# Fillers around the indexer's scores: 24 matmuls ahead of them, five in place of three beside each

## The chip, the cores and the metric

The kernel runs on one core of one Trainium2 chip. The metric is the device time of one execution in microseconds (us), as a median of several runs. The engines are called as in the profile: PE is the matrix engine (TensorE), PEld its weight loads, DVE is VectorE, ACT is ScalarE, POOL is GpSimd and SP is SyncE, which issues most transfers.

## What is computed

One transformer block on 512 tokens of width 1024, all in float32. The part that matters here is the token mixing:

```
q_a,k_a,v_a, q_i,k_i,w_i, q_s,k_s,v_s, g_a,g_b = split(x @ w_in)
# indexer: a score of each key for each query, and its 128 best keys
dots  = einsum('thd,sd->ths', q_i, k_i) * 64**-0.5
score = einsum('th,ths->ts', w_i, relu(dots))            # chunk-causal
sel   = top_k(score, 128)
# branch A: softmax attention over the selected keys, with a relative bias
# branch B: stick-breaking attention, strictly causal
merged = sigmoid(g_a)*(y_a @ w_branch_dsa) + sigmoid(g_b)*(y_s @ w_branch_sb)
x = layer_norm(alpha*x + merged @ w_out)
# then a gated MLP with a causal convolution and a second layer norm
```

Each branch has 8 heads of 64 channels; the indexer has 8 heads of 64.

## The kernel before, in words

**Products.** Each weight and activation is split into a high part (`hi`, made by ACT) and a low part (`lo`, made by DVE, or by POOL or an accumulating transfer for some tiles), and a product is three matmuls: hi by hi, hi by lo, lo by hi. `Stream` loads the weights tile by tile in a fixed order over SP's queue and splits each three tiles ahead of its use (L101 for `whi`, L107 for `wlo`).

**Stages up to the attention.** The indexer's queries are projected while x arrives (L300 to L302). Then come its keys (`idx_keys`, L359), and its scores (`idx_scores`, L377): for each of the query blocks 1, 2 and 3 and each of 8 heads two matmuls of 256, 384 or 512 columns into a PSUM bank `dot_ps` (L385, L386), a relu on ACT (L388) and a multiply and add on DVE (L391, L393). That makes 24 scores of two matmuls. Block 0 has no more than 128 keys and needs none. The top-k of a block (`select`, 16 rounds of a max L402 and a replace L403) runs on DVE. Block 1's rounds are asked for one by one during the scores of blocks 2 and 3; the others behind the scans of the stick-breaking heads (`ROUNDS`).

**Fillers.** All other projections of the token mixing are a list of filler tiles, `FILL` (L33): the stick-breaking values `vs`, then `qs0 ks0 qs1 ks1 qs2 ks2 gb0 gb1` and so on, the sparse branch's values `va`, the output products of branch B (`bs0` to `bs3`) and gates `ga`. A tile of q, k, gate or branch is 24 matmuls of 512 columns; the rest of `vs` is 72 here and `va` 96. `fill(n)` (L607) advances the list by steps of three matmuls until at least n are asked for, so `fill(3)` is one step, `fill(5)` two, `fill(24)` eight. `fill_until(name)` (L614) advances it until a tile is done. Only places in the program move by it: the list and its total stay the same.

**Heads.** `start_head` (L644) asks for a head's q and k tiles and its logits (`z_ps` L503, or `l_ps` for the sparse heads). For a stick-breaking head follow sigmoids on ACT, four scans on DVE (`sb_sticks`, L517), a product on POOL (L519), ten transposes on PE (`tr_ps`, L429), their split (L432, L433) and the product with the values (`av_ps`, L476). Between these steps `fill(GAP)` asks for 15 fillers. The eight sparse heads follow, with the top-k mask added on POOL (`bm`, L532). The values `va` are forced by `fill_until("va")` (L658) at the first of them.

**PSUM.** There are eight banks: four behind `pa` and four behind `pb`. The scores, the keys, all q, k and gate tiles, `va` and `bs` take theirs from `pa`; `vs`, the heads' logits, transposes and products from `pb`.

**What sets the order.** The kernel is built with a planner (L1216, `schedule_with_timeline_sim=True`): it runs the program against its own model of time and puts into each engine's queue, among the instructions that are ready in that model, the one that stands first in the program; `issue_after` ties some behind others. On the chip each queue then runs in that order. So a filler can stand ahead of a score that the program asks for earlier, when the score was not ready in the model, and a place in the program is a priority and not an order.

Of the kernel before, what the change touches and what calls it, by code (L numbers as in the profile page):

```python
# [121 lines left out]
def tile_block(ctx: ExitStack, tc: tile.TileContext, xT, xN, w_qi, w_ki, w_t, w_v, w_br, w_o, w_fi, w_fo,  # L122
# [27 lines left out]
    def pa(name):  # L150
        return psA.tile([128, 512], F32, tag="A", name=name)
# [225 lines left out]
    def idx_scores():  # L377
        kih, kil, wi = index["k"]
        for j in (1, 2, 3):
            N = 128 * (j + 1)  # L380
            for h in range(H):
                yield j
                ps = pa("dot_ps")
                r = slice(j * 128, j * 128 + 128)
                nc.tensor.matmul(ps[:, :N], qi[h][:, r], kih[:, :N], start=True, stop=False)  # L385
                nc.tensor.matmul(ps[:, :N], qi[h][:, r], kil[:, :N], start=False, stop=True)  # L386
                rl = bp.tile([128, 512], F32, tag=("keep", "av", "yt")[h % 3], bufs=2, name="relu")
                nc.scalar.activation(rl[:, :N], ps[:, :N], AF.Relu, scale=0.125)  # L388
                w = wi[:, j - 1, h:h + 1]
                if h == 0:  # L390
                    nc.vector.tensor_scalar(score[j], rl[:, :N], w, None, op0=ALU.mult)  # L391
                else:
                    nc.vector.scalar_tensor_tensor(score[j], rl[:, :N], w, score[j], op0=ALU.mult, op1=ALU.add)  # L393
# [15 lines left out]
    def select_some(n):  # L409
        for _ in zip(range(n), rounds):  # L410
            pass
# [195 lines left out]
    def fill(n):  # L607
        while n > 0:
            c = next(fillers, None)
            if c is None:  # L610
                return
            n -= c
# [15 lines left out]
    for a, b in ((0, 512), (512, NREL)):  # L628
# [6 lines left out]
    nc.gpsimd.dma_start(s_win, bass.AP(tensor=s_line.tensor, offset=s_line.offset + 127,  # L635
                                       ap=[[NREL, H], [-1, 128], [1, 512]]))

    for j in idx_scores():
        if j > 1:
            select_some(1)  # L640
        fill(3)
    heads = [("s", h) for h in range(H)] + [("a", h) for h in range(H)]

    def start_head(i):  # L644
# [575 lines left out]
```

## Time and profile before

| what | us |
|---|---|
| median of 3 runs | 755.36 (754.75 to 755.54) |
| the profiled execution's own time | 754.56 |
| its span, first to last instruction | 752.8 |
| mean granted clock of PE | 0.997 of full speed |
| first score matmul of the indexer | 47.9 |
| first logits of a stick-breaking head (`z_ps`) | 79.6 |
| last product of a sparse head (`av_ps`) ends | 323.0 |

The rest, 323 to 753 us, is the output product, the first norm, the MLP and the second norm. A row of the timeline gives start, length, engine, line, operation, the tiles written and read, the shape, how many like instructions were merged and, in brackets, how long the engine stood idle before it and what ended that. The windows view gives for each stretch its length, then the busy time of PE, PEld, DVE, ACT and POOL with the number of instructions, the granted clock of PE, the busy share of the transfer engines and GB/s. In grouped rows the numbers behind the bar are the busy time in us, the mean of one in ns and the idle time before them.

### The profile page before, as it was taken

Reading aid. Unit: us, or ns where it says so; the run is one execution under the profiler, and the core shown is the slowest. Engines: PE = TensorE matmul, PEld = TensorE weight load, DVE = VectorE, ACT = ScalarE, POOL = GpSimd, SP = SyncE. Lnnn points to the kernel's source line nnn. Section 1 sums busy time; section 2 is a strip of 40 time slices with the busy share of each in tenths; the row PEclk is TensorE's granted clock in tenths of the full one; section 3 lists DMA queues with packets and bytes.
Section 4 is the critical chain, followed back from the end, with each engine's and each line's share of the span. In section 5 each row is a group of like instructions: output and inputs, shape, how many; then the busy total and the mean of one; then the engine's idle time right before and its main releaser. Section 6 shows DMA issues by size and latency. Waiting matters only on the chain.

```text
span 752.8 us, 9797 instructions
## 1 busy us (share of the span) xinstructions
PE 741.5 (99%) x3517; PEld 621.2 (83%) x3517; DVE 567.4 (75%) x906; ACT 397.3 (53%) x572; POOL 137.7 (18%) x162
## 2 busy tenths in 40 slices
PE   9999999999999999999999999999999999999995
PEld 7877888888887888888889888888888888888885
DVE  5569877789889799558774967676776667668985
ACT  6465867675577587746474634443443344346430
POOL 0001224323654231000011111011101101110011
PEclk9999999999999999999999999999999999999998
DMA  8445887673365555317822444435344444448532
GB/s 263 155 125 180 190 202 170 145 169 83 98 157 158 146 126 119 113 57 219 320 53 79 161 148 143 164 113 168 128 153 138 140 149 134 142 149 283 185 134 84
DMA packets 60512, 113.75 MB, mean 151 GB/s; under 512 B 29417, under 2 KB 29673, under 8 KB 60465
## 3 DMA queue, kind: packets, MB, share of 16 engines
q1 hardware_dynamic: 53184, 90.70, 38.7%
q0 software_dynamic: 5744, 18.38, 9.6%
q10 hardware_dynamic: 1536, 4.06, 2.1%
q8 instruction: 27, 0.44, 0.3%
q14 instruction: 21, 0.16, 0.1%
HBM read 95.93 MB, written 9.98 MB: 141 GB/s over the span
## 4 chain that ended last, share of the span: by engine, by line
PE 88%; DVE 7%; ACT 2%; issue 1%; DMA 1%; POOL 0%; SPq 0%; DVEq 0%; ACTq 0%; POOLq 0%
PE u_ps L860 5%; PE u_ps L859 5%; PE g_ps L860 5%; PE u_ps L858 5%; PE g_ps L859 5%; PE g_ps L858 5%; PE m L939 2%; PE m L940 2%; PE m L938 2%; PE av_ps L476 2%; PE ga_ps L228 2%; PE ga_ps L227 2%; PE ga_ps L229 2%; PE o_ps L789 2%; PE o_ps L787 2%; PE o_ps L788 2%
## 5 line engine op out<-in xcount | busy, mean ns | idle before, releaser
L101 ACT ACTIVATE whi<-raw 128x1024 fp32r<-128x1024 f32 (+1 forms) x124 | 124.1, 1002 | 171.5 <-PE g_ps L859 45.5
L107 DVE TENSOR_TENSOR wlo<-raw,whi 128x1024 fp32r<-128x1024 f32 (+1 forms) x105 | 122.7, 1170 | 38.9 <-ACT whi L101 38.1
L860 PE MATMUL u_ps<-x1h,wlo 128*128 128x512 f32 (+1 forms) x192 | 71.4, 372 | 0.0
L858 PE MATMUL u_ps<-x1h,whi 128*128 128x512 f32 (+1 forms) x192 | 71.3, 372 | 0.0
L859 PE MATMUL u_ps<-x1l,whi 128*128 128x512 f32 (+1 forms) x192 | 71.3, 371 | 0.0
L858 PE MATMUL g_ps<-x1h,whi 128*128 128x512 f32 (+1 forms) x184 | 69.9, 380 | 0.0
L859 PE MATMUL g_ps<-x1l,whi 128*128 128x512 f32 (+1 forms) x184 | 69.9, 380 | 0.0
L860 PE MATMUL g_ps<-x1h,wlo 128*128 128x512 f32 (+1 forms) x184 | 69.9, 380 | 0.0
L859 PEld LDWEIGHTS u_ps<-x1l,whi 128*128 128x128 f32 x192 | 36.2, 188 | 6.3
L858 PEld LDWEIGHTS u_ps<-x1h,whi 128*128 128x128 f32 x192 | 36.2, 188 | 6.3
L860 PEld LDWEIGHTS u_ps<-x1h,wlo 128*128 128x128 f32 x192 | 36.2, 188 | 6.2
L859 PEld LDWEIGHTS g_ps<-x1l,whi 128*128 128x128 f32 x184 | 34.6, 188 | 6.6
L858 PEld LDWEIGHTS g_ps<-x1h,whi 128*128 128x128 f32 x184 | 34.6, 188 | 6.5
L860 PEld LDWEIGHTS g_ps<-x1h,wlo 128*128 128x128 f32 x184 | 34.6, 188 | 6.5
L881 DVE TENSOR_TENSOR t<-raw 128x512 f32<-128x512 f32 x11 | 7.6, 692 | 39.9 <-DMA raw<-in_w_fo_dram 39.3
L532 POOL TENSOR_TENSOR bm<-win,score 128x256 f32<-128x256 f32 (+2 forms) x24 | 27.6, 1178 | 33.3 <-DMA pl<-bm 25.9
L914 DVE TENSOR_TENSOR hF<-g_ps,c 128x512 f32<-128x512 f32 x22 | 15.1, 687 | 21.1 <-PE g_ps L860 21.1
L906 ACT ACTIVATE c<-c,cwt 128x512 f32<-128x512 f32 x22 | 15.9, 725 | 25.7 <-DVE c L905 25.5
L900 POOL MEMSET u<- 128x2 f32 x22 | 2.1, 99 | 145.0 <-ACT whi L101 100.8
L402 DVE MAX8 m<-score 128x8 f32<-128x256 f32 (+2 forms) x48 | 26.5, 554 | 0.9
L756 POOL TENSOR_TENSOR rstd<-rstd,mhalf 128x1 f32<-128x1 f32 x8 | 7.7, 959 | 104.4 <-DVE rstd L755 104.4
L519 POOL TENSOR_TENSOR beta<-beta,keep 128x1280 f32<-128x1280 f32 x8 | 19.6, 2453 | 38.9 <-DVE keep L517 30.0
(575 smaller groups left out, 2068.1 us busy)
## 6 DMA issues: line engine op xcount, KB each, us to landing
raw<-in_w_fi_dram SPq DMA_DIRECT2D x44, 512.0 KB, 3.3
raw<-in_w_t_dram SPq DMA_DIRECT2D x32, 512.0 KB, 3.6
raw<-in_w_fo_dram SPq DMA_DIRECT2D x26, 512.0 KB, 4.0
wlo<-in_w_t_dram POOLq DMA_DIRECT2D x14, 512.0 KB, 5.5
raw<-in_w_br_dram SPq DMA_DIRECT2D x8, 512.0 KB, 3.4
raw<-in_w_o_dram SPq DMA_DIRECT2D x8, 512.0 KB, 3.9
raw<-in_w_v_dram SPq DMA_DIRECT2D x7, 512.0 KB, 3.3
raw_b<-in_w_fo_dram SPq DMA_DIRECT2D x6, 512.0 KB, 5.4
```

The lines of the kernel that those rows point to most:

```text
L101: nc.scalar.activation(hi[:, :w], t[:, :w], AF.Copy)
L107: self.done[key] = eng.tensor_sub(lo[:, :w], t[:, :w], r32(hi[:, :w])).ins
L227: nc.tensor.matmul(ps[:M], wh[:, c], xh[k], start=(k == 0), stop=False)
L228: nc.tensor.matmul(ps[:M], wh[:, c], xl[k], start=False, stop=False)
L402: nc.vector.max(m8, sc)
L519: nc.gpsimd.tensor_mul(beta, beta, keep[:, 1:ATT + 1])
L532: nc.gpsimd.tensor_add(bm[:, SOFF[j]:SOFF[j] + N], win[:, 512 - N:512], score[j])
L858: nc.tensor.matmul(ps[:, c], wh[:, kc], x1h[:, k, c], start=(k == 0), stop=False)
L859: nc.tensor.matmul(ps[:, c], wh[:, kc], x1l[:, k, c], start=False, stop=False)
L860: nc.tensor.matmul(ps[:, c], wl[:, kc], x1h[:, k, c], start=False, stop=(k == KC - 1))
L906: nc.scalar.activation(c, c, AF.Gelu_apprx_tanh, bias=cwt[:, f, 3:4])
L914: nc.vector.tensor_mul(F[:, o:o + 2].rearrange("p a b -> p (a b)"), gps_, c)
```

## The change

Two lines in the loop that asks for the scores: 24 fillers are asked for ahead of the first score, and `fill(5)` stands where `fill(3)` stood.

```diff
+    fill(24)
     for j in idx_scores():
         if j > 1:
             select_some(1)
-        fill(3)
+        fill(5)
     heads = [("s", h) for h in range(H)] + [("a", h) for h in range(H)]
```

`idx_scores` yields ahead of each score, so the fillers of one turn stand in the program just ahead of that turn's score. Up to the loop over the heads the program asked for 24 steps of three beside the scores and forced 28 more for the first two pairs of q and k; now it asks for 8 + 48 = 56 steps and those pairs are then complete.

## The prediction

> **What bounds the kernel now.** First the page: engine totals.
>
> ```profile
> span 752.8 us, 9797 instructions
> PE 741.5 (99%) x3517; PEld 621.2 (83%) x3517; DVE 567.4 (75%) x906; ACT 397.3 (53%) x572; POOL 137.7 (18%) x162
> ```
>
> TensorE (PE) is busy 741.5 of 752.8 us. The change adds and removes no matmul; it only asks for some earlier. So it can win no more than the time PE stands still, and the next view, the waits of PE, has two lines that lie behind the edit (waiter, releaser, us, times, longest).
>
> ```profile
> PE dot_ps L385 <- ACT relu L388: 1.0, 1, 1.0
> PE bs_ps L569 <- DVE va L264: 0.9, 1, 0.9
> ```
>
> They are 1.0 us in the indexer's scores (a PSUM bank that ScalarE's relu had not yet read out) and 0.9 us where branch tile bs0 waits for a bank of the `va` projection. Then the windows view, in the order PE, PEld, DVE, ACT, POOL, clock.
>
> ```profile
> 50.00:60.00 10.00, 8.92 (x46) 6.94 (x45) 9.80 (x21) 9.22 (x22) 1.27 (x2) 1.00 0.58 164
> 60.00:70.00 10.00, 10.00 (x45) 8.22 (x44) 9.98 (x24) 5.14 (x9) 1.18 (x5) 1.00 0.47 166
> 200.00:210.00 10.00, 10.00 (x50) 8.50 (x49) 8.03 (x20) 5.39 (x11) 5.94 (x5) 1.00 0.59 157
> 210.00:220.00 10.00, 10.00 (x48) 8.40 (x47) 8.66 (x17) 7.07 (x11) 5.65 (x5) 1.00 0.63 163
> 220.00:230.00 10.00, 9.12 (x42) 7.33 (x41) 9.07 (x15) 8.93 (x15) 5.53 (x6) 1.00 0.79 197
> ```
>
> In 50 to 60 us, the scores, VectorE (9.80) and ScalarE (9.22) are nearly full and PE is idle 1.08 us. VectorE stays full in the next 10 us too (9.98).
>
> **Term 1: the pauses in the scores.** This is PE's timeline through them.
>
> ```profile
> 51.85 0.28 PE L385 MATMUL dot_ps<-kih,qi2a 128*128 128x256 f32 x1
> 51.97 0.28 PE L386 MATMUL dot_ps<-kil,qi2a 128*128 128x256 f32 x1
> ...
> 53.97 0.44 PE L385 MATMUL dot_ps<-kih,qi0a 128*128 128x384 f32 x1 [1.01 <-ACT relu L388]
> ...
> 55.49 0.34 PE L385 MATMUL dot_ps<-kih,qi2a 128*128 128x384 f32 x1
> 55.66 0.34 PE L386 MATMUL dot_ps<-kil,qi2a 128*128 128x384 f32 x1
> ...
> 59.44 0.50 PE L227 MATMUL qs_ps<-xh,whi 128*128 128x512 f32 x1
> ```
>
> From 51.85 to 59.44 us PE issues 32 score matmuls in a row with no filler between them: 8 of 256 columns, 16 of 384, 8 of 512. Undisturbed starts lie 0.12 us apart at 256 columns (51.85 to 51.97) and 0.17 at 384 (55.49 to 55.66); at 512 they are 0.23, as the tile rows of term 2 give. So the 32 need 8 x 0.12 + 16 x 0.17 + 8 x 0.23 = 5.5 us. They took 7.6. PE lost 2.0 us here: the 1.01 us wait and shorter stutters which the page counts as busy, since its rows overlap (0.28 us long at starts 0.12 apart). The value lies between 1.1 (idle time alone) and 2.1; I take 2.0, since the starts are what PE lives by.
>
> [...]
>
> Why no filler stood there: line 641 asks for three filler matmuls ahead of each score, and these come from the rest of `vs`. A build-time planner orders each queue: of the instructions that are ready by its own clock, the earliest in the program goes first. It had used up the `vs` fillers while it waited for the keys, as the grouped rows show: PE from 28.03 us (ahead of the keys' matmuls), then from 38.86 to 47.9 us, where the first score starts.
>
> ```profile
> L256 PE MATMUL vs_ps<-wlo,xh 128*128 128x512 f32 x8 | 3.1, 390 | 0.0
> L257 PE MATMUL vs_ps<-whi,xl 128*128 128x512 f32 x7 | 2.7, 391 | 0.0
> L255 PE MATMUL vs_ps<-whi,xh 128*128 128x512 f32 x8 | 2.6, 391 | 0.0
> ...
> L256 PE MATMUL vs_ps<-wlo,xh 128*128 128x512 f32 x12 | 4.8, 399 | 0.0
> L257 PE MATMUL vs_ps<-whi,xl 128*128 128x512 f32 x12 | 4.7, 390 | 0.0
> L255 PE MATMUL vs_ps<-whi,xh 128*128 128x512 f32 x12 | 4.7, 389 | 0.0
> ```
>
> 23 + 36 = 59 of the 72 `vs` fillers ran ahead of the first score, where the program had asked for 12 + 3. Fillers come in steps of three, so `fill(24)` is 8 steps and `fill(5)` is 2 steps, six matmuls.
>
> - `fill(24)` by itself: 0. Its 24 matmuls are among the 36 that the planner already put between keys and scores.
> - `fill(5)`: the program now asks for 12 + 24 + 24 x 6 = 180 fillers by the last score. 59 are done when the first score is ready, which leaves 121 to lie among the scores. The first two or three scores go at once (12 + 24 + 18 is still under 59), and from there six fillers, 6 x 0.227 = 1.36 us, stand behind each. A relu of 512 columns takes 0.60 us on ScalarE (row below, under Banks), so a bank comes back within that time. The pauses should go: **-2.0 us**.
>
> **Term 2: the head chain moves back.** The fillers are higher in the program than the first head, so its z matmuls now wait for all 180.
>
> ```profile
> 72.34 0.39 PE L227 MATMUL qs_ps<-xh,whi 128*128 128x512 f32 x1
> ...
> 77.78 0.39 PE L227 MATMUL ks_ps<-xh,whi 128*128 128x512 f32 x1
> ...
> 79.60 1.43 PE L503 MATMUL z_ps<-ks0a,qs0a 128*128 128x512 f32 x8
> ```
>
> Between 72.34 and 77.78 us lie the 24 matmuls of one tile: 0.227 us each. Between the first score and the z at 79.60 PE now runs the last 13 `vs` fillers, the 48 of qs0 and qs1, the 24 of ks0 and, from 77.78 to 79.60, 8 of ks1: 93 in all. It will run 121: 28 more, 6.3 us, less the 2.0 us of pauses: the first z comes about 4.3 us later, near 84 us. PE loses nothing by that, since it runs the same work in another order: before, qs1 and ks1 followed the scores; now they stand among them. From head to head the planner's chain (transpose, split, scan, product, transpose) sets a fixed period, so all eight stick-breaking heads and VectorE's top-k rounds, which are tied behind their scans, stay about 4 us late. By the `va` tile the program order is the same again: `fill_until("va")` forces the rest, so the four extra steps ahead of the loop over the heads (24 with the scores and 28 forced by the first two heads before, 8 + 48 = 56 now) drop out and fillers do not run out sooner at the end.
>
> What late heads cost is decided where PE waits for VectorE.
>
> ```profile
> 225.82 0.39 PE L257 MATMUL va_ps<-whi,xl 128*128 128x512 f32 x1
> 227.09 0.50 PE L569 MATMUL bs_ps<-ys0h,whi 128*128 128x512 f32 x1 [0.88 <-DVE va L264]
> ...
> 226.35 2.47 DVE L264 TENSOR_TENSOR va<-va_ps,va 128x512 fp32r<-128x512 f32 x4
> ```
>
> The `va` split stands in VectorE's queue behind the logits of the first sparse heads, which are behind the top-k. In the forecast the planner, finding `va` done before the late logits, puts its split ahead of them, so the wait stays near 0.9: **0**, with bounds -0.9 (gone) and +4.3 (the whole delay arrives).
>
> **Sum.** 754.56 us is the profiled execution's own time (752.8 of span and 1.8 around it); 754.56 - 2.0 = 752.6. The median of the three runs is 755.36, 0.8 above it, so the forecast as a median is 753.4 us. 0.2%, about what a measurement can tell here, is 1.5 us.
>
> **Rivals.**
>
> *Hidden anyway.* The chain of waits that ended last goes through VectorE here, not through PE:
>
> ```profile
> 167.57 1.62 DVE ptl L433 x3
> ...
> 226.43 0.61 DVE va L264
> ```
>  If `va` is split when it is now, PE only reaches the wait at 227 earlier and waits 2.9 us there in place of 0.9. Nothing is won: 755.4. For it: VectorE is 9.07 of 10 busy there. Against it: the planner is free to move the split. That the edit does nothing at all would give the same number; `fill(24)` alone is of that kind.
>
> *The late chain arrives.* VectorE's idle time in 200 to 230 us is 30 - 8.03 - 8.66 - 9.07 = 4.2 us. If half of it can be used up, 4.3 - 2.1 = 2.2 us of the delay are left when bs0 wants its bank; PE's own lead is lost in the same wait, and all behind it is 2.2 us later: 754.56 + 2.2 + 0.8 = 757.5. It decides as soon as more delay is left than the scores gave. Against it: after `va` PE has bs0 and bs1, 96 matmuls, to run while the heads catch up.
>
> *Banks.* The q and k tiles use the same four banks (`pa`) as the scores; `vs` did not. While one tile accumulates and the last is read out, two are left for scores. And ScalarE can be held by the tile's copy:
>
> ```profile
> 60.97 0.60 ACT L388 ACTIVATE relu<-dot_ps 128x512 f32<-128x512 f32 x1 [0.61 <-DVE score L391]
> ...
> 73.48 1.06 ACT L101 ACTIVATE whi<-raw 128x1024 fp32r<-128x1024 f32 x1 [4.12 <-DVE m L402]
> ```
>
> At 73.48 ScalarE had stood 4.12 us behind a copy that needs a split of a full VectorE, harmless now since the relus were over. If each of the four tiles qs0, ks0, qs1, ks1 brings one wait like the 1.01 us one, that is +4.0 - 2.0 = +2.0: 757.4. Against it: a score comes only every 1.36 us of fillers and 2 x 0.23 us of its own.
> [...]
>
> **Chances.** Forecast 0.48 (faster; its own range 752.5 to 754.4, from both waits gone to 1.1 us won); hidden or no effect 0.27; late chain 0.15; banks 0.10. So faster by over 0.2%: 0.47; within: 0.28; slower: 0.25. The range takes in both slower cases and 0.4 us, half the spread of the three runs, at either end: 752.1 to 757.8.
>
> **What would show it.** Right: no run of score matmuls without fillers after the third score; PE busy 10.0 in 50 to 60 us; first z near 84 us, its successors each about 4 us late; `dot_ps <- ACT relu` gone from PE's waits; `bs_ps <- DVE va` near 0.9. Hidden: the scores clean, but that wait near 2.9. Late chain: that wait over 2.9, and the chain of waits on VectorE to about 229 us. Banks: PE waits on relu or on splits of qs and ks between 55 and 84 us. I would be wrong throughout if the first z stayed near 80 us, or if new PE waits came in the sparse heads from 230 to 320 us.

## The result and the profile after

| | median us | runs | lowest to highest |
|---|---|---|---|
| before | 754.70 | 6 | 754.03 to 755.54 |
| after | 765.95 | 6 | 762.34 to 767.66 |

The ratio is 1.0139, with a 95% interval of 1.0112 to 1.0166: the change costs 11.2 us, where 2 us of gain were forecast. The profiled execution of after took 765.8 us with a span of 764.0. Its totals:

```profile
span 764.0 us, 9793 instructions
PE 745.9 (98%) x3517; PEld 625.0 (82%) x3517; DVE 563.1 (74%) x906; ACT 396.6 (52%) x572; POOL 139.6 (18%) x162
```

The span grew by 11.2 us and PE's busy time by 4.4 for the same 3517 matmuls, so some of them ran slower. The waits of PE (us in total, times, longest):

```profile
PE z_ps L503 <- DVE ks0a L328: 3.4, 1, 3.4
PE bs_ps L569 <- DVE va L264: 3.3, 1, 3.3
PE qs_ps L227 <- ACT relu L388: 1.3, 1, 1.3
...
PE ks_ps L227 <- ACT relu L388: 0.7, 1, 0.7
```

The wait of 1.0 us of a score on its relu is gone, as hoped. In its place stand a wait of the first logits for a split (3.4 us, new), two waits of q and k tiles for banks that scores held (2.0 together), and the wait of bs0 for the `va` split, 3.3 where it was 0.9. The windows (PE, PEld, DVE, ACT, POOL, then the granted clock):

```profile
50.00:60.00 10.00, 9.27 (x48) 7.69 (x47) 6.67 (x12) 6.43 (x14) 2.02 (x2) 1.00 0.59 162
60.00:70.00 10.00, 10.00 (x47) 8.46 (x46) 3.41 (x5) 5.85 (x11) 1.79 (x4) 1.00 0.65 226
70.00:80.00 10.00, 6.58 (x26) 5.49 (x25) 9.50 (x27) 3.91 (x7) 1.91 (x3) 0.80 0.83 222
...
230.00:240.00 10.00, 6.74 (x25) 5.37 (x25) 8.73 (x16) 7.51 (x15) 7.08 (x7) 0.83 0.71 187
```

From 60 to 70 us VectorE works 3.41 of 10 us, where it had been full (9.98). It is full again from 70 us, when PE stands. Both stretches in which PE stands also show a clock below 1 (0.80 and 0.83). PE's timeline through both:

```profile
72.79 0.33 PE L386 MATMUL dot_ps<-kil,qi3b 128*128 128x384 f32 x1
76.55 1.33 PE L503 MATMUL z_ps<-ks0a,qs0a 128*128 128x512 f32 x3 [3.42 <-DVE ks0a L328]
...
81.62 0.63 PE L227 MATMUL ks_ps<-xh,whi 128*128 128x512 f32 x1
82.05 0.63 PE L228 MATMUL ks_ps<-xl,whi 128*128 128x512 f32 x1
...
83.83 0.39 PE L228 MATMUL ks_ps<-xl,whi 128*128 128x512 f32 x1
84.06 0.40 PE L229 MATMUL ks_ps<-xh,wlo 128*128 128x512 f32 x1
...
233.00 0.39 PE L257 MATMUL va_ps<-whi,xl 128*128 128x512 f32 x1
236.64 0.80 PE L569 MATMUL bs_ps<-ys0h,whi 128*128 128x512 f32 x1 [3.26 <-DVE va L264]
237.23 0.63 PE L570 MATMUL bs_ps<-ys0l,whi 128*128 128x512 f32 x1
```

Behind each of the two waits matmuls of 512 columns start 0.43 us apart (81.62 to 82.05), against 0.23 a little later (83.83 to 84.06): half speed, for 6.3 us behind the first wait (76.55 to 82.9) and 3.3 us behind the second (236.64 to 239.97). The granted clock reads 0.50 from 76.5 to 82.5 us and from 236.5 to 239.5. Half of such a stretch is lost.

Why z waited is told by the chain that ended last (start, us, what):

```profile
50.30 16.27 DMA s_win<-s_line
66.58 2.61 DMA win<-s_win
...
70.10 0.44 DVE m L402
...
75.81 0.69 DVE ks0a L328
76.55 1.33 PE z_ps L503 x3
...
214.76 0.34 DVE score L405
215.10 0.07 issue
215.17 1.30 POOL bm L532
...
235.99 0.61 DVE va L264
236.64 0.80 PE bs_ps L569
```

The first half starts at the relative-bias windows, which no score needs. They are built by a transfer on GpSimd's queue, and the memsets that finish them stand in that queue too; there the two kernels differ. GpSimd's timeline, before and then after:

```profile
58.23 0.14 POOL L399 MEMSET score<- 64x64 f32 x1 [6.70 <-DVE score L393]
68.25 0.14 POOL L528 MEMSET win<- 64x64 f32 x1 [9.87 <-DMA win<-s_win]
```

```profile
69.25 0.14 POOL L528 MEMSET win<- 64x64 f32 x1 [7.76 <-DMA win<-s_win]
69.83 0.14 POOL L528 MEMSET win<- 64x64 f32 x1 [0.45 <-DMA win<-s_win]
69.92 0.14 POOL L399 MEMSET score<- 64x64 f32 x1
```

L399 masks the invalid keys of block 1 and opens its top-k. Before, it ran at 58.23, ahead of the memsets of the windows. After, the planner, with the scores spread further, put it behind them, and it ran at 69.92, 11.7 us later. The queue made 8.2 us of that: VectorE had finished block 1's scores at 61.8 us. The rest is the wider spread of the scores. VectorE's queue had the max rounds next and stood 6.55 us behind it, with the split of `ks0` queued behind the rounds (75.81 in the chain). VectorE's timeline:

```profile
70.10 0.43 DVE L402 MAX8 m<-score 128x8 f32<-128x256 f32 x1 [6.55 <-POOL score L399]
```

And the first head did not go on when z was done. ScalarE's timeline, before and then after:

```profile
82.47 0.60 ACT L507 ACTIVATE keep<-z_ps 128x512 f32<-128x512 f32 x1 [2.09 <-DVE m L402]
```

```profile
96.33 0.60 ACT L388 ACTIVATE relu<-dot_ps 128x512 f32<-128x512 f32 x1 [3.44 <-PE dot_ps L386]
96.82 0.59 ACT L507 ACTIVATE keep<-z_ps 128x512 f32<-128x512 f32 x1
```

The first sigmoid (L507) stands behind the relu of the last score, at 96.8 us where before had it at 82.5. Its tile `keep` shares its two buffers with every third relu. So the first transposes come at 107.9 us in place of 92.7, the last head's at 206.9 (194.5) and the end of the third top-k (L405) at 214.7. VectorE's timeline before has it at 202.3:

```profile
202.34 0.43 DVE L405 TENSOR_SCALAR score<-score 128x512 f32<-128x512 f32 x1
```

From there the second half of the chain runs: the end of the top-k frees the mask add on GpSimd, that the logits, and behind those in VectorE's queue stands the `va` split. When the last product of the sparse heads starts (333.7 against 322.7) after is 11 us behind and stays so.

### The profile page after: what moved, and what is told of

It reads as the page before. It is cut to its first block, busy times and chain, and to the rows that moved or that the text cites. A ratio compares the mean times of both kernels' runs of the same rounds, so it can differ in the third digit from the quotient of the medians.

```text
span 764.0 us, 9793 instructions
## 1 busy us (share of the span) xinstructions
PE 745.9 (98%) x3517; PEld 625.0 (82%) x3517; DVE 563.1 (74%) x906; ACT 396.6 (52%) x572; POOL 139.6 (18%) x162
## 3 DMA queue, kind: packets, MB, share of 16 engines
HBM read 95.93 MB, written 9.98 MB: 139 GB/s over the span
## 4 chain that ended last, share of the span: by engine, by line
PE 81%; DVE 8%; DMA 4%; issue 3%; ACT 2%; POOL 1%; SPq 0%; DVEq 0%; ACTq 0%; POOLq 0%
PE u_ps L859 5%; PE u_ps L861 5%; PE g_ps L859 5%; PE u_ps L860 5%; PE g_ps L861 5%; PE g_ps L860 5%; PE m L940 2%; PE m L941 2%; PE m L939 2%; DMA s_win<-s_line 2%; PE ga_ps L228 2%; PE ga_ps L227 2%; PE av_ps L476 2%; PE ga_ps L229 2%; PE o_ps L789 2%
## 5 line engine op out<-in xcount | busy, mean ns | idle before, releaser
L532 POOL TENSOR_TENSOR bm<-win,score 128x256 f32<-128x256 f32 (+2 forms) x24 | 30.9, 1313 | 32.6 <-DMA pl<-bm 28.7
```

The lines of the kernel that those rows point to most:

```text
L532: nc.gpsimd.tensor_add(bm[:, SOFF[j]:SOFF[j] + N], win[:, 512 - N:512], score[j])
```

## The experiments

Two theories at the start. *Queue*: the cost is the mask's place in GpSimd's queue, and the rest follows. *Late heads*: the heads start late whatever that queue does, and VectorE's top-k carries the lateness to the `va` split, so what is won in the scores comes back as wait there. Medians in us and ratios to before (754.7 to 755.5 in the five groups of runs):

| run | median | ratio, 95% interval |
|---|---|---|
| after + mask ahead (e1) | 767.13 | 1.0143 (1.0124 to 1.0163) |
| after + mask on VectorE (e2) | 766.72 | 1.0142 (1.0121 to 1.0163) |
| fill(24) alone (e3) | 760.53 | 1.0057 (1.0036 to 1.0077) |
| fill(5) alone (e4) | 761.11 | 1.0062 (1.0040 to 1.0084) |
| before, MLP pools swapped (e5) | 760.58 | 1.0075 (1.0063 to 1.0088) |
| fill(24), pools swapped (e6) | 755.54 | 1.0012 (1.0003 to 1.0022) |
| e1 + relus leave `keep` (e7) | 759.42 | 1.0060 (1.0046 to 1.0074) |
| e9 with twelve rounds (e8) | 754.91 | 1.0004 (0.9995 to 1.0013) |
| e1, pools swapped (e9) | 764.10 | 1.0118 (1.0104 to 1.0132) |
| e9 + rounds first (e10) | 756.82 | 1.0025 (1.0016 to 1.0034) |
| fill(5), pools swapped (e11) | 757.52 | 1.0034 (1.0022 to 1.0047) |
| before + rounds first (e12) | 753.12 | 0.9975 (0.9965 to 0.9984) |
| after + rounds first (e13) | 759.56 | 1.0058 (1.0045 to 1.0072) |
| e6 + rounds first (e14) | 753.57 | 0.9976 (0.9968 to 0.9985) |
| e11 + rounds first (e15) | 755.22 | 1.0002 (0.9991 to 1.0013) |

**The mask ahead of the windows (e1) and on VectorE (e2).**

```diff
+    masked = {}
...
-        nc.gpsimd.memset(sc[0:64, N - 64:N], INVALID)
+        masked[j] = nc.gpsimd.memset(sc[0:64, N - 64:N], INVALID).ins
...
-        nc.gpsimd.memset(win[0:64, 448:512], BIG)
+        with tc.issue_after(masked[1]):
+            nc.gpsimd.memset(win[0:64, 448:512], BIG)
```
```diff
-        nc.gpsimd.memset(sc[0:64, N - 64:N], INVALID)
+        nc.vector.memset(sc[0:64, N - 64:N], INVALID)
```

> The changed kernel with one tie added: in GpSimd's queue the memsets of the sparse heads' windows stand behind the memset of block 1's score. Theory Q (the queue): in the changed kernel that score memset stood behind two window memsets which wait for the window transfer, so VectorE waited 6.6 us for it, its queue was late, and PE waited 3.4 us for the split of ks0 and then ran some 5 us at half clock. Without it: no DVE wait on L399 over 1 us, no PE wait at the first z, and 5 to 7 us less than the changed kernel, near 759 to 761 us; nearer to 756 if the wait at va (3.3 us) shrinks too. Theory L (late heads): the loss at the end is set by how late the heads are, whatever made them late; the wait at va grows by what the first one gives up, and the time stays within 2 us of the changed kernel's 765.95. Rival B (banks): the PE waits on relu (1.3 and 0.7 us) stay in both cases and are no more than 2 us.

> The changed kernel with the memset of the future keys' scores on VectorE in place of GpSimd, so that the top-k cannot wait for GpSimd's queue at all. Theory Q: as e1, within 1 us of it, less some 0.3 us of added VectorE work. Theory L: within 2 us of the changed kernel.

Neither gained. The longest waits of PE in e1:

```profile
PE bs_ps L572 <- DVE va L264: 6.8, 1, 6.8
PE u_ps L862 <- DVE hF L918: 3.0, 1, 3.0
```

The wait of z was gone and the first logits came at 73.2 us, but the first sigmoid only at 90.6, the third top-k ended at 212.6, and the wait at `va` grew from 3.3 to 6.8 us. That speaks for late heads. The mask itself ran at 62.2 us, right behind its scores. The second line is a wait far away, in the MLP, that neither kernel of the comparison has; e2 has it as well.

**One half at a time (e3, e4).** e3 is after with `fill(3)` again, e4 is after without `fill(24)`.

> fill(24) is added and fill(3) is kept. The prediction: no effect, 754.7 within 1.5 us. Theory Q: the planned queue of GpSimd has the score memset ahead of the window memsets here, so no 6.6 us wait, and the time is within 2 us of before. Theory L: the eight added steps end the scores some 5 us later, so the first z and the transposes are about 5 us late; if lateness alone costs, the wait at va grows from 0.9 to 2 or 3 us and the time to 756 to 758.

> fill(5) without fill(24). Theory Q: the score memset stands ahead of the window memsets in GpSimd's planned queue, so no 6.6 us wait; the scores' 2.0 us of pauses are mostly filled; 752.5 to 756. Theory L: 48 steps stand with the scores in place of 24, of which 16 come ahead of the first head anyway; the scores end 10 us later or more, the heads with them, and the time is 757 to 762.

Each costs 5 to 6 us, by the waits of PE (e3, then e4) largely through the MLP wait again:

```profile
PE u_ps L859 <- DVE hF L915: 3.0, 1, 3.0
PE bs_ps L569 <- DVE va L264: 2.2, 1, 2.2
```

```profile
PE u_ps L858 <- DVE hF L914: 2.9, 1, 2.9
PE qs_ps L227 <- ACT relu L388: 1.2, 1, 1.2
...
PE dot_ps L385 <- ACT relu L388: 1.0, 1, 1.0
PE bs_ps L569 <- DVE va L264: 0.9, 1, 0.9
```

In e3 the scores' waits on relu also rise a little, from 1.0 us to 1.5.

**The MLP wait is an accident of banks (e5, e6).** The first u and g tiles of the MLP take the four `pa` banks in whatever rotation the attention left them. The next u tile takes the first bank of a pool opened afterwards, bank 4. In the program as built, g of f=1 stands in bank 6 in before and 7 in after, but in bank 4 in e1 to e4, and there u waits 2.9 to 3.0 us until VectorE has read it. Opening the two pools in the other order gives u bank 6:

```diff
-    psc, psC = open_pool("psC", space=PSUM, reuse_waits="tile")
-    psd, psD = open_pool("psD", space=PSUM, reuse_waits="tile")
+    psd, psD = open_pool("psD", space=PSUM, reuse_waits="tile")
+    psc, psC = open_pool("psC", space=PSUM, reuse_waits="tile")
...
```

> The kernel before with the two PSUM pools of the MLP opened in the other order, so that u of f=2 takes bank 6, where g of f=1 stands in this build, in place of bank 4, where g of f=0 stands. Bank theory (the 3.0 us MLP wait that the four earlier runs have, and neither kernel of the comparison, is the accident of which bank g of f=1 drew): a PE wait of u_ps on DVE's hF of 2.9 to 3.1 us appears and the time is 754.7 + 3.0 = 757.7 us. Rival (that wait comes from the changed order of work ahead of the MLP): no such wait, 754.7.

> fill(24) alone, with the two PSUM pools opened in the other order; g of f=1 stood in bank 4 there, and u of f=2 now takes bank 6. Bank theory: the 3.0 us MLP wait is gone and the time is 760.5 - 3.0 = 757.5 us, which is what fill(24) by itself costs. Rival (the wait comes from the changed order): 760.5 again.

The bank theory holds both ways: before acquires the wait (3.0 us in e5), e3 loses it (none in e6). PE's timeline in e5:

```profile
422.13 0.39 PE L860 MATMUL g_ps<-x1h,wlo 128*128 128x512 f32 x1
425.50 0.69 PE L858 MATMUL u_ps<-x1h,whi 128*128 128x512 f32 x1 [2.98 <-DVE hF L914]
425.99 0.63 PE L859 MATMUL u_ps<-x1l,whi 128*128 128x512 f32 x1
426.41 0.63 PE L860 MATMUL u_ps<-x1h,wlo 128*128 128x512 f32 x1
```

On before and on e3 it cost more than its 3.0 us, 5.5 and 5.0; half speed can follow it here too (starts 0.42 us apart, 425.99 to 426.41). On e4 and e1 it cost 3.6 and 3.0 (e11 and e9 below). Free of it, fill(24) alone costs 0.5 us: PE comes to the last `va` matmul half a microsecond earlier than before (225.3 against 225.8) and waits 2.2 us there in place of 0.9.

**What makes the heads late (e7).** e1 with the relus kept out of the `keep` buffers:

```diff
-                rl = bp.tile([128, 512], F32, tag=("keep", "av", "yt")[h % 3], bufs=2, name="relu")
+                rl = bp.tile([128, 512], F32, tag=("av", "yt")[h % 2], bufs=2, name="relu")
```

> The kernel after, with the top-k mask ahead of the windows' memsets as in the first run, and the relus of the scores in the buffers av and yt only, so that the first head's keep tile no longer waits for relus of the last scores; g of f=1 does not stand in bank 4 or in the bank that u of f=2 takes. Late-heads theory: first keep sigmoid near 80 us in place of 90.6, first transposes near 92 (101.6), third top-k end near 202 (212.6), the wait of bs0 on va under 1.5 us (6.8), time 753.5 to 755.5 us. Rival A (the 24 and 5 fillers cost PE in the scores whatever the heads do): 764 us, which is the first run without its MLP wait. Rival B (four relu buffers in place of six hold the scores up): PE waits on relu of 2 us or more between 50 and 95 us, 757 or more.

```profile
PE dot_ps L385 <- DVE qs1b L338: 3.4, 1, 3.4
PE bs_ps L572 <- DVE va L264: 1.7, 1, 1.7
```

The heads came early as expected (first sigmoid 75.3 us, first transposes 87.3), so the shared buffers were what held the first head, and the wait at `va` fell to 1.7. But a late score now stood 3.4 us behind the split of qs1, the last score started at 97.1 and the third top-k ended at 207.2, not 202. The forecast of 753.5 to 755.5 was missed by 4 us, and by the trace this new wait accounts for most of that: PE stood 3.4 us for it. What half speed added is not shown apart; the mean clock of the profiled execution (760.5 us) was 0.992, that of the other four (759.1 to 759.8) 0.995 to 0.998, and that of before 0.996 to 0.998. The heads are also not the only thing ahead of the top-k; the scores themselves are.

**VectorE's top-k carries the lateness (e8, e9, e10).** e9 is e1 with the pools swapped, the base of the other two. e8 leaves out four of the 16 rounds of each top-k, so that it selects fewer keys; e10 leaves out nothing and only asks for the rounds earlier:

```diff
-        for _ in range(NSEL // 8):
+        for _ in range(NSEL // 8 - 4):
```
```diff
-ROUNDS = 3, 3, 4, 5, 5, 6, 6
+ROUNDS = 6, 6, 6, 6, 4, 2, 2
```

> The kernel after, with the mask ahead and the two PSUM pools in the other order, and with 12 rounds of max and match_replace in each of the three top-k selections in place of 16: 12 rounds, about 14 us of VectorE, are left out. Theory that VectorE's top-k carries the lateness to the va split: the wait of bs0 on va falls from 6.8 us to under 1, bs0 starts near 226, and the time is 767.1 - 3.0 - 6.8 = 757.3 us or up to 2 less (the half clock behind the wait). Rival (the chain of heads, one period each, carries it, whatever the top-k takes): the last head's transposes stay near 204 us, the wait stays over 4, 761 to 764 us.

> The first run (after, with the top-k mask ahead of the windows' memsets) with the two PSUM pools of the MLP in the other order. Bank accident as measured in the two swapped runs (5.0 and 5.5 us each): 767.1 - 5.2 = 761.9 us, so that the mask's place in GpSimd's queue is worth 4 us of the 11, where the first run seemed to show nothing. Rival (the queue wait is worth nothing, and the wait in the MLP was hidden there): 766 to 767.

> As the run beside it, with the top-k rounds behind the heads dealt out as 6, 6, 6, 6, 4, 2, 2 in place of 3, 3, 4, 5, 5, 6, 6: nothing is left out, and VectorE's work is the same, only earlier, in its idle time behind the first heads. Top-k theory: the third top-k ends 8 us earlier or more (212.6 in the first run), the wait of bs0 on va falls from 6.8 us to under 2, time 755 to 757 us. Rival (the chain of heads carries the lateness; its last transposes at 204 us stay): wait over 4, 760 to 762. Second rival (rounds ahead of the splits hold the first heads up): first and last transposes later than 101.6 and 204.2, 762 or more.

PE's waits in e8 have no line of bs0 any more. In e9 and in e10 it reads:

```profile
PE bs_ps L572 <- DVE va L264: 6.8, 1, 6.8
```

```profile
PE bs_ps L572 <- DVE va L264: 2.4, 1, 2.4
```

e10 is the clean one: the first and last transposes stay where they were (101.3 and 203.3 us, against 100.7 and 203.9 in e9), so the chain of heads is as late as ever. The third top-k ends 11 us earlier (201.2 against 212.3), the wait falls by 4.4 us and the time by 7.3. So the end of the top-k sets most of the wait, and the rival that the heads carry all of it by themselves falls. The 2.4 us that stay, where under 2 were expected, are not explained by the top-k, which ends earlier here than in before (202.3); the heads, still 9 us late, may carry them, which no run separates. The time falls by more than the wait. Half speed can account for some of that: the mean clock is 0.991 to 0.993 in all executions of e9, and 0.996 or 0.997 in those of e10 that took 756 to 757 us (its profiled one, at 0.993, took 759.2). e8 agrees, 9.2 us less than e9 and a little below its own forecast, but there the last transposes came earlier too, so it separates less.

e9 itself is 1.9 us quicker than after (764.10 and 765.95). That is not the 4 expected, and it lies within the spread of after's executions (762.3 to 767.7): what the mask's place wins in the scores mostly comes back at `va`, where the wait rises from 3.3 us to 6.8. So the theory of the queue falls as an account of the whole, and that of the late heads stands for what the runs without the mask's delay still cost.

**fill(5) alone, and rounds first on the others (e11 to e15).**

> fill(5) alone with the two PSUM pools in the other order. Bank theory: the 3.0 us MLP wait goes and 5.0 to 5.5 us with it: 761.1 - 5.2 = 755.9 us, which is what fill(5) by itself costs. If it stays over 758, fill(5) has a cost of its own that the waits of the first run did not show.

> The kernel before with the rounds dealt out as 6, 6, 6, 6, 4, 2, 2. Top-k theory: bs0's wait on va (0.9 us) goes, and PE has nothing else to wait for there: 754.9 - 0.9 = 754.0 us (faster by 0.1%). Rival (what PE gains there is lost at the next late result in the sparse heads): 754.9. Third case (rounds hold the heads' scans up, so that the last transposes come after 194.5): 756 or more.

> The kernel after itself, with only the top-k rounds behind the heads dealt out as 6, 6, 6, 6, 4, 2, 2. If the stalls in the scores (9.4 us between 58 and 90 us) and the wait at va are two costs that add up: the wait of bs0 on va falls from 3.3 us to under 1 and the half clock behind it (1.9) goes, the stalls stay, time 766.0 - 3.3 - 1.9 = 760.8 us (760 to 762). If the late heads were all of it and the stalls are swallowed by that wait: 755 to 757. If the heads are too late for earlier rounds to help: wait stays over 3, 765 or more.

> fill(24) alone, PSUM pools of the MLP in the other order, rounds 6, 6, 6, 6, 4, 2, 2. Its profile without the rounds showed PE at the end of va 0.5 us earlier than before and a wait of 2.2 us there, with half clock behind it. Top-k theory: the wait goes, 755.5 - 2.2 = 753.3 us or down to 752.2 with the half clock gone, as fast as the kernel before with the same rounds (753.1). Rival (fill(24) costs something elsewhere): 754.5 or more.

> fill(5) alone, PSUM pools of the MLP in the other order, rounds 6, 6, 6, 6, 4, 2, 2. Its profile without the rounds showed 1.7 us of wait at va and 2.2 us of waits on relu in the scores. Top-k theory: the wait at va goes, 757.5 - 1.7 = 755.8 us or up to 1 less; if the waits on relu go too, which the earlier rounds give no reason for, 753.6. Rival (five fillers cost by another way than late heads): 757 or more.

The waits of PE in e12, and then in e13:

```profile
PE idle_ps L204 <- DVE idle L201: 1.2, 1, 1.2
PE dot_ps L385 <- ACT relu L388: 1.0, 1, 1.0
```

```profile
PE z_ps L503 <- DVE ks0a L328: 3.5, 1, 3.5
PE qs_ps L227 <- ACT relu L388: 1.3, 1, 1.3
```

With the rounds asked for early, the wait at `va` is gone from both, while the stalls of after in the scores stand as they were. So in after there are two costs. 759.56 - 753.12 = 6.4 us is the price of the stalls in the scores, and the other 11.2 - 6.4 = 4.8 us, uncertain by some 2 us because after itself spreads, came through the late top-k. From the trace of after: 3.4 us of z's wait, half of the 6.3 us behind it, 2.0 us of waits on relu, less the 2.0 that the forecast found as pauses before, make 6.6. At `va` 2.4 us more of wait and half of the 3.3 us behind it make 4.1.

The two are not independent. e10 has the mask ahead and the rounds first, and none of z's wait. It is 2.7 us quicker than e13 and still 3.7 slower than e12, since PE now comes earlier to `va` and waits 2.4 us there. Of the stall in the scores a part only takes the place of a later wait.

e12 gained 1.9 us on before, twice the wait of 0.9 that went; where the rest came from is not traced. e14 confirms that fill(24) alone costs nothing clear of the noise but its wait at `va` (753.57 beside 753.12). e11 and e15 show that fill(5) alone costs 2 us of its own (757.52, and 755.22 beside 753.12), which no earlier top-k removes: the 1.0 us wait of a score stays, and a wait of a q tile on relu of 1.2 us comes with it. e12 and e14 beat both kernels of the comparison, by 0.25% over before.

## Why the prediction was wrong, point by point

- **What bounds the kernel** was right: PE, and after the edit the two places where PE waits, the scores and the `va` split.
- **fill(24) by itself: 0.** The number was nearly right for that line alone (0.5 us), but by luck, since its reason was wrong. The planner put about as many `vs` fillers ahead of the first score as before (57 counted in e6, 59 in before), and the 24 stood among the scores: 61 fillers between the first and the last score where before had 37, and the last score at 71.7 us where it was 66.6. What hid the cost was the way of the rival *Hidden anyway*: PE came half a microsecond earlier to a split that came no earlier. Beside fill(5) its eight steps move the last score back, from 84.9 us in e11 to 88.5 in e9 and, with the stalls, 96.6 in after; the pair costs 11.2 us where the halves cost 0.5 and 2.5.
- **fill(5): the pauses go, -2.0.** One did: the run of scores without fillers, with its 1.0 us wait, is gone from after. But q and k tiles wait on relu for 2.0 us instead. That is the mechanism of the rival *Banks*, for two tiles of its four. In e11 both kinds stand.
- **"PE loses nothing by that"** is the first step that failed. The forecast let z wait for all 180 fillers, 121 of them behind the first score, near 84 us. In the trace of after 85 ran ahead of it (93 in before) and 16 of the 48 score matmuls were still to come: the planner had put it there, at 76.6, where its operand was not ready on the chip. The forecast looked at PE's queue alone. It did not follow the mask through GpSimd's queue past the windows' memsets, nor the split of ks0 behind the rounds in VectorE's. Together with the waits on relu of the point above this is 6.4 of the 11.2 us, by e13 against e12.
- **The head chain 4.3 us later** was mis-sized. z came earlier, yet the first sigmoid came 14.4 us later (96.8 against 82.5), because the first head's `keep` shares buffers with the relus and stands behind the last of them; e7 shows that. The last transposes were 12.4 us late. The "fixed period" held: a lateness of 15.2 us at the first head was still 12.4 at the last.
- **The wait of bs0 on `va`: 0.** This is the second step that failed. "The planner, finding `va` done before the late logits, puts its split ahead of them" did not happen: the split stayed behind three heads' logits. The rival *The late chain arrives* named this place and its sign, and priced it for 2.2 us out of 4.3; about 12 arrived. The split then came 9.6 us late (235.9 against 226.35) and PE itself 7.2 us late (233.0 against 225.8), which left 2.4 us of wait plus half speed, some 4.8 by e13.
- No term of the forecast was for half speed behind a wait. Of the 11.2 us some 5 are that: half of 6.3 us behind z and half of 3.3 behind bs0.

What stays open: why the planner's clock put the mask behind the windows in after and not in e3 or e4, where it ran at 57.3 and 57.5 us. GpSimd stood 7.76 us at that memset, which suggests that the planner expected the transfer sooner, but this was only argued. What fill(5) alone costs (2 us) is located, in waits on relu, and not further split.

## What to carry to other kernels

A place in a program that a planner orders is not a place in the queue: for each step that an edit moves, follow the instruction on every engine that prepares it, above all behind a wait for a transfer on a queue that nothing seems to depend on. A pause on the engine that bounds the kernel may be paid back at a later wait, and so may what is won by filling it: find the first point where the late chain meets the bound engine, and give that chain its work earlier (here, a third top-k that ends 11 to 14 us sooner took away 0.9 to 4.4 us of wait, and 1.9 to 7.3 us of time). Before a difference of a few us is put down to an edit, look for a wait far from it that came or went by which buffer a tile drew.

## What the runs showed of the hardware

- The profiles here have 15 waits of PE of 2.2 to 6.8 us behind the start of the scores. In after the clock stood at half from 76.1 to 82.9 us around the end of z's wait (3.4 us, until 76.55) and from 236.5 to 239.9 around that of bs0's (3.3 us, until 236.64). At the wait of bs0 the clocks of the windows, taken as a mix of 1 and 0.50, put half speed in e1 (6.8 us) from 232.5 to 239.3 us, in e10 (2.4 us) from 228.2 to 235.0 and in e6 (2.2 us) from 229.4 to 232.8, an estimate; whole windows inside these stretches read 0.50 in e1 and e10, and in e6 230 to 233 us reads 0.53. Behind u's wait of 3.0 us in e5 the matmuls of 512 columns took 0.63 to 0.69 us up to the start at 428.55, and start 0.42 to 0.49 us apart, against 0.39 and 0.23 ahead of it. Behind the 3.0 of e1, the 3.0 of e3 and the 2.9 of e4 no matmul of u took more than 0.51 us up to 450 us. For the other six there is only the mean clock of the profiled execution: 0.988 in e2 (6.7 and 3.0 us), 0.992 in e7 (3.4), 0.991 in e9 (6.8), 0.993 in e13 (3.5), and in e3 (2.2) 0.997, as in before, where no wait is over 1.2 us. The length of a wait alone does not tell here whether half speed comes: 2.2 us in e6 had it, 3.0 in e1 and e3 not. Executions of one kernel spread with the granted clock: after ran 762.3 and 763.0 us at 0.994, 766.9 and 767.7 at 0.989.
- The transfer that builds the windows in DRAM, 2 MB read at shifted offsets, took 16.3 us in after (15.2 in before). GpSimd's queue stood 7.76 us at the memset of a window that is read from it, and the mask behind that memset, whose scores were done at 61.8 us, ran at 69.92.
